# One gather of 96 slots for main and overflow tokens in a top-4-of-32 expert layer

## The chip, the cores and the metric
The kernel runs on one core of one Trainium2 chip. The metric is the device time of one execution in microseconds (us). A core has five engines with instruction streams of their own, TensorE (PE; its weight loads are listed apart as PEld), VectorE (DVE), ScalarE (ACT), GpSimd (POOL) and SyncE (SP), which wait for each other through semaphores. SyncE issues nearly all transfers here.

## The reference
One decoder layer for 256 tokens of 1024 values: an input projection, two kinds of attention, an output projection, a layer norm, and then a sparse feed-forward layer, which is what the change touches:

```
logits = h @ w_router + b_router          # 256 x 32
top_val, top_idx = top_k(logits, 4)
gates = softmax(top_val)
for each expert e, for its tokens:
    u = h @ w_up[e] + b_up[e]             # 1024 -> 2048, interleaved gate and up
    gate = min(u[::2], 7); up = clip(u[1::2], -7, 7)
    act = (up + 1) * gate * sigmoid(1.702 * gate)
    y[token] += gates * (act @ w_down[e] + b_down[e])
out = layer_norm(alpha * h + y)
```

All values are float32. An expert's weights are 12.58 MB (two halves of w_up and w_down, 4.19 MB each), all 32 experts' 403 MB.

## The kernel before
The first 235 us of the profiled execution hold the mixer and the router. The rest is one unrolled loop over the 32 experts, `for e in range(NE)` (L928), and then the second layer norm (`second_norm`, L1039).

**Slots.** Each expert has room for S = 64 tokens in its main pass. Tokens beyond that go to an overflow pass of Q = 32 slots, and a rare block, `general()` (L887), takes what exceeds 96 (and expert 0's overflow). `place` (L713) makes, from a token's rank among its expert's tokens, a 0/1 matrix `ph` (tokens by slots) on VectorE; `gather` (L736) multiplies the tokens, split in three bfloat16 parts (`hs`), with it on TensorE, 8 x 2 x 3 = 48 matmuls, and copies the result to `xg`, tokens' values by slots.

**One expert.** In the order of TensorE: `up` with the first half of w_up (L948); in odd experts `ways_back`; `up` with the second half (L961 or L968), each half of 32 matmuls of 512 columns by the profile; `swiglu` on VectorE and ScalarE beside it; the gather for the *next* expert (L978), whose copy VectorE makes; in even experts `combine`, which adds two experts' results to the four accumulators `y`; two transposes of `act` (L991) into `pts` (L988), one in the bank of `h0`, one in the two-deep ring `m`; the gates of the next expert's slots (`slot_gates`, L994) into the same bank as the second transpose; ScalarE's two copies to `actT` (L992, L995), the second behind the gates; then `down` (L1013) and its drain `keep_two` by ScalarE and VectorE.

**Conditionals.** Between the copies and `down` stands the first conditional, `is_over(e + 1)` (L1000): if the next expert overflows, place its overflow tokens, gather them, compute their gates, run `up` on the weights that are there and `swiglu`. Behind `down` stands the second, `is_over(e)` (L1019): place the way back on GpSimd (`place_back`), then `more_down` and `more_back`. Behind expert 30 stands the third, `words[4] > 0` (L1030), with the rare block of 32 conditionals with loops. Every engine has its own copy of each branch and tests a register of its own. The body of a conditional lies in the program behind the path that skips it: where it isn't entered, a branch goes past it.

**Weights.** Five slots of 4.19 MB form a ring (`ring`, L82). `load(k)` (L84) fills slot k % 5 with part k (three an expert) by SyncE; expert e issues the loads of parts 3e + 5 and 3e + 6, half by half, when `up` has read the part that was in the slot, and of part 3e + 7 behind both conditionals. The rare block reloads weights into one slot (`SLOT`, L926), the one of the down weights of the expert that it stands behind.

**PSUM.** Eight banks: four accumulators `y`, `h0`, `h1`, and the ring `m` of two, which the gather, the second transpose, `down` and others take in turn.

Of the kernel before, what the change touches and what calls it, by code (L numbers as in the profile page):

```python
# [9 lines left out]
F32 = mybir.dt.float32  # L10
# [21 lines left out]
def tile_hybrid(ctx, tc, x, w_in, w_o, lambda_qk, subln_g, sinks, ln_g, ln_b,  # L32
# [12 lines left out]
    def pool(stack, name, side="right", **kw):  # L45
# [2 lines left out]

    ident = keep.tile([128, 128], F32, name="ident")
    make_identity(nc, ident)  # L50
    iota_s = keep.tile([128, S], F32, name="iota_s")
    nc.gpsimd.iota(iota_s, pattern=[[1, S]], base=-int(NOT_HERE), channel_multiplier=0,
                   allow_small_or_imprecise_dtypes=True)
    iota_e = keep.tile([128, NE], F32, name="iota_e")
    nc.gpsimd.iota(iota_e, pattern=[[1, NE]], base=0, channel_multiplier=0, allow_small_or_imprecise_dtypes=True)
# [677 lines left out]
        nc.vector.tensor_reduce(gs, p, AX.X, OP.add)  # L733
        return gs

    def gather(ph, n, p=None, xg=None, copy=nc.scalar.copy):  # L736
        p = pm.tile([128, 8, n], F32, name="p", tag="m") if p is None else p
        for j in range(8):
            for tt in range(2):
                for k in range(3):  # L740
                    nc.tensor.matmul(p[:, j, :], hs[:, tt, k, j, :], ph[:, tt, :],  # L741
                                     start=(tt == 0 and k == 0), stop=(tt == 1 and k == 2))
        xg = mp.tile([128, 8, n], F32, name="xg", tag="xg") if xg is None else xg
        copy(xg, p)
        return xg

    halves = [slice(r * S, (r + 1) * S) for r in range(2)]
# [25 lines left out]
    def up(e, n, b, h, xg, u, js):  # L773

        G = 128 // n

        def cols16(t, q):
            o = 16 // G * q + 4 * b
            return t.rearrange("p (i r) -> p i r", r=16)[:, :, o:o + 4]

        if js[0] == 0:
            for q in range(G):
                nc.tensor.matmul(h[q * n:(q + 1) * n], sel[:, e:e + 1].to_broadcast([96, n]), cols16(bups, q),  # L783
                                 start=True, stop=False, tile_position=(0, q * n))
        for j in js:
            for q in range(G):
                nc.tensor.matmul(h[q * n:(q + 1) * n], xg[:, j, :], cols16(u[:, j % 4, :], q),  # L787
                                 start=False, stop=(j == 7), tile_position=(0, q * n))

    def swiglu(h, act, gs, tmp=None):  # L790
# [89 lines left out]
    gm3 = mp.tile([128, 2, NE, 3], BF, name="gm3", bufs=1)  # L880
    rankT = mp.tile([NE, 2, 128], BF, name="rankT", bufs=1)
    xg_of, gs_of = {}, {}
    ph = place(rankp[:, :, 0], S)
    xg_of[0] = gather(ph, S)
    ph_0 = ph
    nc.sync.dma_start(out=bd, in_=b_down[0])
    def general():  # L887

        d = ring[SLOT]
        df = d.rearrange("p j c -> p (j c)")  # L890
        act2 = mp.tile([128, 2, 128], F32, name="more")
        actT2 = mp.tile([128, 2, 128], F32, name="moreT", tag="actT0", bufs=1)
        yb2 = mp.tile([128, 512], F32, name="yb2", bufs=1)
        pgt2 = mp.tile([128, 2, 128], F32, name="pgt2", tag="actT1", bufs=1)
        pg2 = mp.tile([128, 2, 4, Q], F32, name="pg2", tag="pg", bufs=1)
        rk = mp.tile([128, 2], F32, name="rk")
        ph2 = mp.tile([128, 2, Q], BF, name=f"ph{Q}")
        xg2 = mp.tile([128, 8, Q], F32, name="xg", tag="xg")
        gs2 = mp.tile([128, 1], F32, name="gs")
        tmp = [mp.tile([128, 2, 128], F32, name=k, **kw) for k, kw in (("g", {"bufs": 1}), ("sg", {"bufs": 1}), ("u", {"bufs": 1}))]  # L900
        m = [pm.tile([128, 512], F32, name=f"m{k}", tag="m") for k in range(2)]
        three = [m[k].rearrange("p (a b) -> p a b", b=128)[:, 0:2] for k in range(2)]
        for e in range(NE):
            def again(i):
                nc.scalar.dma_start(out=df, in_=_rows(w_up, 128, e * D * 2048 + i * 8192, 16384, 8192))
                return d.rearrange("p (j a) c -> p j (a c)", a=2)

            with is_over(e, 1 if e else 0):
                nc.vector.tensor_scalar(rk, rankp[:, :, e], float(S if e else S - Q), None, op0=OP.subtract)
                n = nc.values_load(extra[:, e:e + 1], min_val=1, max_val=NX,  # L910
                                   skip_runtime_bounds_check_because="a count of at most 256 tokens")
                with tc.For_i(1 if e else 0, n, 1):
                    nc.vector.tensor_scalar(rk, rk, float(Q), None, op0=OP.subtract)
                    place_back(pg2, rk, 4, Q)
                    place(rk, Q, ph2)
                    gather(ph2, Q, m[0].rearrange("p (a b) -> p a b", b=Q)[:, 0:8], xg2)
                    slot_gates(ph2, e, Q, m[0][:, 256:259], gs2)
                    h2 = m[1].rearrange("p (i a b) -> p i a b", a=2, b=2)
                    for i in range(2):
                        up(e, Q, 0, h2, xg2, again(i), range(4 * i, 4 * i + 4))  # L920
                    swiglu(h2, act2, gs2, tmp)
                    nc.scalar.dma_start(out=df, in_=_rows(w_down, 128, e * D * D, 8192, 8192))
                    more_down(d, act2, actT2, pg2, pgt2, yb2, three + [m[0]])
                    more_back(pgt2, yb2)

    SLOT = (3 * (NE - 2) + 2) % 5  # L926
    act2_of = {}
    for e in range(NE):  # L928
        par = e % 2
        u0, u1, d = weights(e)  # L930
# [6 lines left out]
            elif k < 3 * NE:  # L937
                load(k, range(2 * half, 2 * half + 2), 4) if k > 3 * NE - 8 else load(k, (half,), 2)

        ph = place(rankp[:, :, e + 1], S) if e + 1 < NE else None  # L940
        if e == 0:
            counts()
            gates()
# [1 line left out]
        h = [h_tile(0), h_tile(1)]  # L945
        for j in range(4):
            for b in range(2):
                up(e, S, b, h[b], xg_of[e], u0, (j,))  # L948
            if j % 2:
                load_some(3 * e + 5, j // 2)  # L950
        if e == 0:
            turn_ranks()
            gs_of[0] = slot_gates(ph_0, 0, S, pm.tile([128, 3], F32, name="ps", tag="m"))
            words = [nc.values_load(over[:, k:k + 1], skip_runtime_bounds_check_because="a word of 16 flags")
                     for k in range(5)]
        if par == 1:
            wb = ways_back(e)
        if e < NE - 2:
            for b in range(2):
                for j in (4, 6):  # L960
                    up(e, S, b, h[b], xg_of[e], u1, (j, j + 1))  # L961
                    if b:
                        load_some(3 * e + 6, j // 2 - 2)
                swiglu(h[b], act[b], gs_of[e])
        else:
            for j in range(4, 8):
                for b in range(2):
                    up(e, S, b, h[b], xg_of[e], u1, (j,))  # L968
                if j % 2:
                    load_some(3 * e + 6, j // 2 - 2)  # L970
            for b in range(2):
# [3 lines left out]
            for k in range(2):  # L975
                nc.sync.dma_start(out=tail[:, k, :], in_=_rows((ln_g, ln_b)[k], 128, D, 0, D))
        if e + 1 < NE:
            xg_of[e + 1] = gather(ph, S, copy=nc.vector.tensor_copy)  # L978
        if par == 0 and e > 0:
            combine(wb)  # L980
        if e == NE - 1:
# [3 lines left out]
                for r in range(2):  # L985
                    nc.gpsimd.memset(part[halves[r], :, (1 - r) * 256:(2 - r) * 256].bitcast(F32), 0.0)  # L986
        actT = [mp.tile([128, 2, 128], F32, name=f"actT{b}", bufs=1) for b in range(2)]
        pts = [pm.tile([128, 512], F32, name="pt", tag="h0", bufs=1), pm.tile([128, 512], F32, name="pt", tag="m")]  # L988
        pt = [t[:, :256].rearrange("p (a b) -> p a b", b=128) for t in pts]
        for b in range(2):  # L990
            trans(act[b], pt[b])  # L991
        nc.scalar.copy(actT[0], pt[0])  # L992
        if e + 1 < NE:
            gs_of[e + 1] = slot_gates(ph, e + 1, S, pts[1][:, 256:259])  # L994
        nc.scalar.copy(actT[1], pt[1])  # L995
        if e == NE - 4:
            add_b_down()
# [1 line left out]
        if e + 1 < NE:  # L999
            with is_over(e + 1):  # L1000
                act2_of[e + 1] = mp.tile([128, 2, 128], F32, name="more")
                rk = mp.tile([128, 2], F32, name="rk")
                nc.vector.tensor_scalar(rk, rankp[:, :, e + 1], float(S), None, op0=OP.subtract)
                ph2 = place(rk, Q)
                p = pm.tile([128, 512], F32, name="p", tag="h0", bufs=1)
                xg2 = gather(ph2, Q, p[:, :256].rearrange("p (a b) -> p a b", b=Q))
                gs2 = slot_gates(ph2, e + 1, Q, p[:, 256:259])
                h2 = h_tile(0)
                for i, u in enumerate(weights(e + 1)[:2]):
                    up(e + 1, Q, 0, h2, xg2, u, range(4 * i, 4 * i + 4))  # L1010
                swiglu(h2, act2_of[e + 1], gs2)
        if e < NE - 1:
            p = down(d, S, actT, swap=par)  # L1013
# [3 lines left out]
            last_down(d, actT)  # L1017
        if e > 0:
            with is_over(e):  # L1019
                rk = mp.tile([128, 2], F32, name="rk")  # L1020
                nc.vector.tensor_scalar(rk, rankp[:, :, e], float(S), None, op0=OP.subtract)
                pg2 = mp.tile([128, 2, 4, Q], F32, name="pg2", tag="pg", bufs=1)
                place_back(pg2, rk, 4, Q)
                actT2 = mp.tile([128, 2, 128], F32, name="moreT", tag="actT0", bufs=1)
                yb2 = mp.tile([128, 512], F32, name="yb2", bufs=1)
                pgt2 = mp.tile([128, 2, 128], F32, name="pgt2", tag="actT1", bufs=1)
                more_down(d, act2_of[e], actT2, pg2, pgt2, yb2)
                more_back(pgt2, yb2)
        if e == NE - 2:
            with tc.If(words[4] > 0, preferred_fallthrough_block=False):  # L1030
                general()
        load(3 * e + 7)
# [53 lines left out]
```

## Time and profile before

| | us |
|---|---|
| median of 3 runs | 1237.45 (1232.15 to 1239.41) |
| profiled execution | 1235.14 |
| its span, first to last instruction | 1233.3 |
| TensorE matmuls busy | 1091.3 (88%) |
| VectorE, ScalarE, GpSimd busy | 364.1, 219.4, 104.0 |
| mean granted TensorE clock | 0.963 |
| read from memory | 438.72 MB, 357 GB/s over the span |

The span is what the trace covers; the execution's own time is 1.84 us more. Matmul ends are modelled, so a busy TensorE isn't TensorE at its peak. "issue" as the end of a wait means that the profile shows nothing that the engine waited for; an engine name with a q is that engine's sequencer, which branches and waits while the engine stands idle.

### The profile page before, as it was taken

The page shows a single profiled execution, that of the slowest core. Times are in us where ns is not written, and L with a number is a line of the kernel's source. Part 1 is how long each engine was busy: PE and PEld are TensorE (multiplying, and loading weights), DVE is VectorE, ACT ScalarE, POOL GpSimd, SP SyncE. Part 2 cuts the span into 40 slices and gives each one's busy share as a digit, 9 for nine tenths or more (in the row PEclk, how much of TensorE's full clock was granted, in tenths as well). Part 3 has the DMA queues.
Part 4 walks back from the last instruction along what each step waited for, and adds up shares of the span by engine and source line. Part 5 has one row for each costly group of instructions (what it writes and reads, how often), then busy time and mean ns, then how long its engine had stood idle before and what let it go on. Part 6 is the DMA issues. An engine that isn't in the chain of part 4 may idle for free. (4 is left out here: it accounts for less than half of the span.)

```text
span 1233.3 us, 17816 instructions
## 1 busy us (share of the span) xinstructions
PE 1091.3 (88%) x7027; PEld 545.3 (44%) x7027; DVE 364.1 (30%) x782; ACT 219.4 (18%) x458; POOL 104.0 (8%) x104
## 2 busy tenths in 40 slices
PE   8999999797999998779899998877899998898965
PEld 7989685332434343323343433332333433353322
DVE  4555964622122222111212122211122221222104
ACT  4765661301001001100001000000001100000001
POOL 1066561200000000000000000000000000000002
PEclk9999999899999999999999999989999999899988
DMA  9932537778899999997999999999999999999940
GB/s 333 380 123 104 196 113 297 297 295 368 337 408 426 425 425 425 412 399 323 375 425 425 426 426 425 427 425 428 426 424 426 426 426 427 424 425 420 418 180 35
DMA packets 46607, 441.80 MB, mean 358 GB/s; under 512 B 5121, under 2 KB 8321, under 8 KB 20513
## 3 DMA queue, kind: packets, MB, share of 16 engines
q1 hardware_dynamic: 46320, 439.52, 86.1%
q8 instruction: 104, 1.70, 0.6%
q14 instruction: 39, 0.31, 0.1%
q10 hardware_dynamic: 144, 0.26, 0.1%
HBM read 438.72 MB, written 1.05 MB: 357 GB/s over the span
## 5 line engine op out<-in xcount | busy, mean ns | idle before, releaser
L787 PE MATMUL h<-w,xg 128*64 128x512 f32 (+1 forms) x2176 | 476.5, 600 | 3.5 <-issue 2.4
L814 PE MATMUL pd<-w,actT 128*64 128x512 f32 x992 | 242.5, 638 | 64.5 <-issue 42.8
L787 PEld LDWEIGHTS h<-w,xg 128*64 128x64 f32 (+1 forms) x2176 | 167.0, 136 | 267.2 <-issue 255.2
L814 PEld LDWEIGHTS pd<-w,actT 128*64 128x64 f32 x992 | 84.9, 147 | 200.4 <-issue 184.3
L822 DVE TENSOR_TENSOR yl<-pd,yh 64x512 fp32r<-64x512 f32 (+1 forms) x66 | 44.4, 672 | 351.0 <-ACT yh L821 332.8
L796 ACT ACTIVATE sg<-g 128x256 f32<-128x256 f32 x66 | 27.6, 417 | 473.2 <-DVE g L795 473.2
L795 DVE TENSOR_SCALAR g<-h 128x256 f32<-128x256 f32 x66 | 28.0, 425 | 252.7 <-PE h L787 252.7
L821 ACT CAST yh<-pd 64x512 fp32r<-64x512 f32 (+1 forms) x66 | 37.4, 566 | 324.6 <-PE pd L814 294.1
L164 POOL TENSOR_TENSOR lo<-w,hi 128x1024 fp32r<-128x1024 f32 x31 | 78.9, 2553 | 103.4 <-ACT hi L163 103.3
L741 PEld LDWEIGHTS <-hs 128*128 128x128 bf16 x1632 | 50.3, 99 | 28.1 <-issue 24.5
L986 POOL MEMSET yh<- 64x512 f32 x2 | 1.0, 518 | 689.3 <-PE y L844 689.2
L741 PE MATMUL p<-ph,hs 128*128 128x64 bf16 (+1 forms) x1632 | 54.2, 194 | 2.8 <-DVE ph L717 2.8
L163 ACT CAST hi<-w 128x1024 fp32r<-128x1024 f32 x48 | 50.2, 1045 | 19.5 <-PE pj L202 13.8
L783 PE MATMUL h<-biases,sel 96*64 96x512 bf16 (+1 forms) x136 | 28.8, 410 | 27.6 <-ACT yh L821 16.4
L191 PE MATMUL pj<-xh,hi 128*128 128x256 f32 x272 | 40.8, 294 | 1.3 <-ACT gbt L516 0.7
L759 DVE TENSOR_SCALAR wb<-p,slot 128x512 fp32r<-128x512 f32 x16 | 12.0, 751 | 98.1 <-PE p L756 98.1
L191 PE MATMUL pj<-xl,hi 128*128 128x256 f32 x272 | 39.0, 287 | 0.0
L191 PE MATMUL pj<-xh,lo 128*128 128x256 f32 x272 | 39.0, 287 | 0.0
L191 PEld LDWEIGHTS pj<-xh,hi 128*128 128x128 f32 x272 | 36.0, 196 | 3.6 <-issue 1.0
L783 PEld LDWEIGHTS <-sel 96*64 96x64 bf16 (+1 forms) x136 | 9.3, 108 | 62.9 <-PEq L1019 41.6
L191 PEld LDWEIGHTS pj<-xh,lo 128*128 128x128 f32 x272 | 35.9, 196 | 0.0
L191 PEld LDWEIGHTS pj<-xl,hi 128*128 128x128 f32 x272 | 35.9, 196 | 0.0
(240 smaller groups left out, 829.1 us busy)
## 6 DMA issues: line engine op xcount, KB each, us to landing
w<-in_w_up_dram SPq DMA_DIRECT2D x120, 2048.0 KB, 22.3
w<-in_w_down_dram SPq DMA_DIRECT2D x58, 2048.0 KB, 23.2
w<-in_w_in_dram SPq DMA_DIRECT2D x5, 4096.0 KB, 15.6
w<-in_w_up_dram SPq DMA_DIRECT2D x16, 1024.0 KB, 21.2
w<-in_w_down_dram SPq DMA_DIRECT2D x12, 1024.0 KB, 20.8
w<-in_w_o_dram SPq DMA_DIRECT2D x2, 2048.0 KB, 10.9
w<-in_w_in_dram SPq DMA_DIRECT2D x1, 2048.0 KB, 14.4
w<-in_w_in_dram SPq DMA_DIRECT2D x1, 1536.0 KB, 9.6
```

The costliest lines, as they stand in the source:

```text
L163: nc.scalar.copy(hi, src)
L164: by.tensor_sub(lo, src, hi)
L191: nc.tensor.matmul(p[:, :256], a[:, j, :], b[:, j, :], start=(j == 0 and n == 0), stop=(j == 7 and n == 2))
L741: nc.tensor.matmul(p[:, j, :], hs[:, tt, k, j, :], ph[:, tt, :], start=(tt == 0 and k == 0), stop=(tt == 1 and k == 2))
L759: nc.vector.tensor_scalar(wb.rearrange("p k a b -> p k (a b)"), p, slot[:, 0:1], None, op0=OP.is_equal)
L783: nc.tensor.matmul(h[q * n:(q + 1) * n], sel[:, e:e + 1].to_broadcast([96, n]), cols16(bups, q), start=True, stop=False, tile_position=(0, ...
L787: nc.tensor.matmul(h[q * n:(q + 1) * n], xg[:, j, :], cols16(u[:, j % 4, :], q), start=False, stop=(j == 7), tile_position=(0, q * n))
L795: nc.vector.tensor_scalar(g, gt, 7.0, None, op0=OP.min)
L796: nc.scalar.activation(sg, g, AF.Sigmoid, scale=1.702)
L814: nc.tensor.matmul(p[r * n:(r + 1) * n, :w], actT[c // 2][:, c % 2, q * n:(q + 1) * n], d[:, k, o * w:(o + 1) * w], start=(k == 0), stop=( ...
L821: nc.scalar.copy(yh[at], p)
L822: nc.vector.tensor_sub(yl[at], p, yh[at])
```

## The change
The gather of an expert makes S + Q = 96 columns in place of 64, so that the overflow tokens are gathered along with the others, for every expert, whether it overflows or not. Its result takes two banks of the ring `m` (four groups of 96 columns, at a pitch of 128, in each) and two copies; the gathered tile is single, not double. The first conditional loses its placement and its gather, and gets the `place_back` of the second. The second transpose moves from the ring `m` to the bank of `h1`. The rare block moves from behind expert 30 to behind expert 24 (`LATE`), and some tiles of the blocks get other buffers.

```diff
-    def gather(ph, n, p=None, xg=None, copy=nc.scalar.copy):
-        p = pm.tile([128, 8, n], F32, name="p", tag="m") if p is None else p
-        for j in range(8):
+    def gather(ph, p):
+        for j, pj in enumerate(p):
             for tt in range(2):
                 for k in range(3):
-                    nc.tensor.matmul(p[:, j, :], hs[:, tt, k, j, :], ph[:, tt, :],
+                    nc.tensor.matmul(pj, hs[:, tt, k, j, :], ph[:, tt, :],
                                      start=(tt == 0 and k == 0), stop=(tt == 1 and k == 2))
-        xg = mp.tile([128, 8, n], F32, name="xg", tag="xg") if xg is None else xg
-        copy(xg, p)
+
+    def gather_all(ph, copy):
+        p = [pm.tile([128, 4, 128], F32, name="p", tag="m") for k in range(2)]
+        gather(ph, [p[j // 4][:, j % 4, :S + Q] for j in range(8)])
+        xg = mp.tile([128, 8, S + Q], F32, name="xg", bufs=1)
+        for k in range(2):
+            copy(xg[:, 4 * k:4 * k + 4], p[k][:, :, :S + Q])
         return xg
...
-    SLOT = (3 * (NE - 2) + 2) % 5
-    act2_of = {}
+    LATE = 24
+    SLOT = (3 * LATE + 2) % 5
+    act2_of, pg2_of = {}, {}
...
-        ph = place(rankp[:, :, e + 1], S) if e + 1 < NE else None
+        ph = place(rankp[:, :, e + 1], S + Q) if e + 1 < NE else None
+        xg = [xg_of[e][:, j, :S] for j in range(8)]
...
-            xg_of[e + 1] = gather(ph, S, copy=nc.vector.tensor_copy)
+            xg_of[e + 1] = gather_all(ph, nc.vector.tensor_copy)
...
-        pts = [pm.tile([128, 512], F32, name="pt", tag="h0", bufs=1), pm.tile([128, 512], F32, name="pt", tag="m")]
+        pts = [pm.tile([128, 512], F32, name="pt", tag=f"h{b}", bufs=1) for b in range(2)]
...
             with is_over(e + 1):
                 act2_of[e + 1] = mp.tile([128, 2, 128], F32, name="more")
+                pg2_of[e + 1] = mp.tile([128, 2, 4, Q], F32, name="pg2")
                 rk = mp.tile([128, 2], F32, name="rk")
                 nc.vector.tensor_scalar(rk, rankp[:, :, e + 1], float(S), None, op0=OP.subtract)
-                ph2 = place(rk, Q)
-                p = pm.tile([128, 512], F32, name="p", tag="h0", bufs=1)
-                xg2 = gather(ph2, Q, p[:, :256].rearrange("p (a b) -> p a b", b=Q))
-                gs2 = slot_gates(ph2, e + 1, Q, p[:, 256:259])
+                place_back(pg2_of[e + 1], rk, 4, Q)
                 h2 = h_tile(0)
                 for i, u in enumerate(weights(e + 1)[:2]):
-                    up(e + 1, Q, 0, h2, xg2, u, range(4 * i, 4 * i + 4))
+                    up(e + 1, Q, 0, h2, [xg_of[e + 1][:, j, S:] for j in range(8)], u, range(4 * i, 4 * i + 4))
+                gs2 = slot_gates(ph[:, :, S:], e + 1, Q, pm.tile([128, 3], F32, name="p", tag="h1", bufs=1))
                 swiglu(h2, act2_of[e + 1], gs2)
...
             with is_over(e):
-                rk = mp.tile([128, 2], F32, name="rk")
-                nc.vector.tensor_scalar(rk, rankp[:, :, e], float(S), None, op0=OP.subtract)
-                pg2 = mp.tile([128, 2, 4, Q], F32, name="pg2", tag="pg", bufs=1)
-                place_back(pg2, rk, 4, Q)
...
-                more_down(d, act2_of[e], actT2, pg2, pgt2, yb2)
+                more_down(d, act2_of[e], actT2, pg2_of[e], pgt2, yb2)
                 more_back(pgt2, yb2)
-        if e == NE - 2:
+        if e == LATE:
             with tc.If(words[4] > 0, preferred_fallthrough_block=False):
                 general()
```

## Rows read from the trace of the kernel before

**Rows 1.** The page: one DMA queue (packets, MB, share of 16 engines).
```profile
q8 instruction: 104, 1.70, 0.6%
```

**Rows 2.** Waits, whole span (who <- whom: us in total, times, longest).
```profile
PE pd L814 <- issue: 42.8, 13, 6.5
PE h L783 <- issue: 8.4, 1, 8.4
PE pd L814 <- DMA w<-in_w_up_dram: 6.6, 1, 6.6
PE h L787 <- DMA w<-in_w_up_dram: 1.0, 1, 1.0
...
SPq L99 <- PE h L787: 315.1, 95, 9.1
```

**Rows 3.** Branches of L1000, L1019, L1030 on TensorE (ns min/median/max, first and last us).
```profile
L1000 PEldq COMPARE_BRANCH  x60: 66/238/6142, 256.6 to 1171.5; - x60
L1019 PEldq COMPARE_BRANCH  x60: 66/187/404, 300.4 to 1221.9; - x60
L1030 PEldq COMPARE_BRANCH  x2: 71/3614/7157, 1182.5 to 1183.0; - x2
```

**Rows 4.** Windows around entered blocks (first, second, first): busy us (x instructions) by engine.
```profile
257.95:269.28 11.33, 10.46 (x124) 3.89 (x124) 0.24 (x2) 0.37 (x1) 0.00 (x0) 0.85 0.67 282
303.60:317.95 14.35, 9.29 (x79) 4.32 (x80) 3.22 (x8) 2.26 (x5) 1.20 (x2) 0.88 0.36 133
468.60:479.44 10.84, 8.97 (x124) 3.51 (x124) 0.28 (x2) 0.37 (x1) 0.00 (x0) 1.00 1.01 425
```

**Rows 5.** Timeline of TensorE, four starts of an expert, one gather, one hole.
```profile
675.49 0.42 PE L783 MATMUL h<-biases,sel 96*64 96x512 bf16 x2 [0.73 <-ACT yh L821]
...
702.39 0.42 PE L783 MATMUL h<-biases,sel 96*64 96x512 bf16 x2 [0.73 <-ACT yh L821]
...
717.20 1.57 PE L741 MATMUL p<-ph,hs 128*128 128x64 bf16 x48
...
728.41 0.42 PE L783 MATMUL h<-biases,sel 96*64 96x512 bf16 x2 [0.73 <-ACT yh L821]
...
749.39 8.56 PE L814 MATMUL pd<-w,actT 128*64 128x512 f32 x32 [2.55 <-issue]
...
758.68 0.42 PE L783 MATMUL h<-biases,sel 96*64 96x512 bf16 x2 [0.73 <-ACT yh L821]
```

**Rows 6.** Windows: the same columns, then clock, DMA share, GB/s.
```profile
549.00:553.30 4.30, 0.00 (x0) 0.00 (x0) 0.00 (x0) 0.00 (x0) 0.00 (x0) 0.73 0.99 419
553.30:558.00 4.70, 4.63 (x12) 1.62 (x14) 0.00 (x0) 0.00 (x0) 0.00 (x0) 0.52 0.69 289
235.00:345.00 110.00, 98.18 (x738) 39.88 (x740) 28.63 (x94) 13.49 (x27) 1.20 (x2) 0.94 0.83 343
520.00:600.00 80.00, 65.35 (x416) 27.20 (x418) 14.19 (x34) 6.20 (x14) 0.00 (x0) 0.91 0.85 350
600.00:1180.00 580.00, 518.20 (x3227) 218.52 (x3225) 123.82 (x287) 53.60 (x118) 0.00 (x0) 0.96 1.00 423
```

**Rows 7.** Groups by line and shape: VectorE's drain (busy us, mean ns).
```profile
L744 DVE COPY xg<-p 128x512 f32<-128x512 f32 x31 | 21.2, 685 | 0.0
```

**Rows 8.** Timeline in the two blocks that are entered for one expert.
```profile
258.03 1.35 PE L741 MATMUL p<-ph,hs 128*128 128x32 bf16 x48 [1.07 <-DVE ph L717]
...
260.39 0.41 PE L783 MATMUL h<-biases,sel 96*32 96x512 bf16 x4 [0.34 <-DVE gs L733]
...
308.36 0.42 DVE L767 COPY pgt<-p 128x256 f32<-128x256 f32 x1 [1.72 <-PE p L765]
```

**Rows 9.** Timeline and one window of the tail.
```profile
1200.95 7.09 PE L787 MATMUL h<-w,xg 128*64 128x512 f32 x32
...
1221.88 1.30 DVE L1041 BATCH_NORM_STATS2 st<-y 128x6 f32<-128x512 f32 x2 [0.92 <-PEq L1019]
...
1188.00:1192.00 4.00, 1.66 (x6) 0.74 (x8) 0.00 (x0) 0.00 (x0) 0.00 (x0) 0.50 0.34 132
```

More of the change, by code (lines that the diff above doesn't have):

```diff
@@ L50, in tile_hybrid @@
     make_identity(nc, ident)
-    iota_s = keep.tile([128, S], F32, name="iota_s")
-    nc.gpsimd.iota(iota_s, pattern=[[1, S]], base=-int(NOT_HERE), channel_multiplier=0,
+    iota_s = keep.tile([128, S + Q], F32, name="iota_s")
+    nc.gpsimd.iota(iota_s, pattern=[[1, S + Q]], base=-int(NOT_HERE), channel_multiplier=0,
                    allow_small_or_imprecise_dtypes=True)
@@ L786, in up @@
             for q in range(G):
-                nc.tensor.matmul(h[q * n:(q + 1) * n], xg[:, j, :], cols16(u[:, j % 4, :], q),
+                nc.tensor.matmul(h[q * n:(q + 1) * n], xg[j], cols16(u[:, j % 4, :], q),
                                  start=False, stop=(j == 7), tile_position=(0, q * n))
@@ L882, in tile_hybrid @@
     xg_of, gs_of = {}, {}
-    ph = place(rankp[:, :, 0], S)
-    xg_of[0] = gather(ph, S)
-    ph_0 = ph
+    ph_0 = place(rankp[:, :, 0], S + Q)
+    xg_of[0] = gather_all(ph_0, nc.scalar.copy)
     nc.sync.dma_start(out=bd, in_=b_down[0])
@@ L894, in general @@
         pgt2 = mp.tile([128, 2, 128], F32, name="pgt2", tag="actT1", bufs=1)
-        pg2 = mp.tile([128, 2, 4, Q], F32, name="pg2", tag="pg", bufs=1)
+        pg2 = mp.tile([128, 2, 4, Q], F32, name="pg2")
         rk = mp.tile([128, 2], F32, name="rk")
         ph2 = mp.tile([128, 2, Q], BF, name=f"ph{Q}")
-        xg2 = mp.tile([128, 8, Q], F32, name="xg", tag="xg")
+        xg2 = mp.tile([128, 8, Q], F32, name="xg2", tag="act0", bufs=1)
         gs2 = mp.tile([128, 1], F32, name="gs")
@@ L915, in general @@
                     place(rk, Q, ph2)
-                    gather(ph2, Q, m[0].rearrange("p (a b) -> p a b", b=Q)[:, 0:8], xg2)
+                    p = m[0].rearrange("p (a b) -> p a b", b=Q)[:, 0:8]
+                    gather(ph2, [p[:, j] for j in range(8)])
+                    nc.scalar.copy(xg2, p)
                     slot_gates(ph2, e, Q, m[0][:, 256:259], gs2)
@@ L919, in general @@
                     for i in range(2):
-                        up(e, Q, 0, h2, xg2, again(i), range(4 * i, 4 * i + 4))
+                        up(e, Q, 0, h2, [xg2[:, j, :] for j in range(8)], again(i), range(4 * i, 4 * i + 4))
                     swiglu(h2, act2, gs2, tmp)
@@ L947, in tile_hybrid @@
             for b in range(2):
-                up(e, S, b, h[b], xg_of[e], u0, (j,))
+                up(e, S, b, h[b], xg, u0, (j,))
             if j % 2:
@@ L952, in tile_hybrid @@
             turn_ranks()
-            gs_of[0] = slot_gates(ph_0, 0, S, pm.tile([128, 3], F32, name="ps", tag="m"))
+            gs_of[0] = slot_gates(ph_0[:, :, :S], 0, S, pm.tile([128, 3], F32, name="ps", tag="m"))
             words = [nc.values_load(over[:, k:k + 1], skip_runtime_bounds_check_because="a word of 16 flags")
@@ L960, in tile_hybrid @@
                 for j in (4, 6):
-                    up(e, S, b, h[b], xg_of[e], u1, (j, j + 1))
+                    up(e, S, b, h[b], xg, u1, (j, j + 1))
                     if b:
@@ L967, in tile_hybrid @@
                 for b in range(2):
-                    up(e, S, b, h[b], xg_of[e], u1, (j,))
+                    up(e, S, b, h[b], xg, u1, (j,))
                 if j % 2:
@@ L993, in tile_hybrid @@
         if e + 1 < NE:
-            gs_of[e + 1] = slot_gates(ph, e + 1, S, pts[1][:, 256:259])
+            gs_of[e + 1] = slot_gates(ph[:, :, :S], e + 1, S, pts[1][:, 256:259])
         nc.scalar.copy(actT[1], pt[1])
@@ L1019, in tile_hybrid @@
             with is_over(e):
-                rk = mp.tile([128, 2], F32, name="rk")
-                nc.vector.tensor_scalar(rk, rankp[:, :, e], float(S), None, op0=OP.subtract)
-                pg2 = mp.tile([128, 2, 4, Q], F32, name="pg2", tag="pg", bufs=1)
-                place_back(pg2, rk, 4, Q)
                 actT2 = mp.tile([128, 2, 128], F32, name="moreT", tag="actT0", bufs=1)
```

## The prediction

> **What bounds the kernel now.** I read the waits first. TensorE hardly ever waits for weights: the longest wait that is truly one is 1.0 us [rows 2]. The transfers wait for TensorE instead: the queue that loads weights sat 315.1 us until the up matmuls had freed a slot [rows 2]. So the order of work on TensorE sets the end, and its holes are worth their length, until the weights themselves come too late.
>
> The holes have one place. Thirteen times the down projection (L814) started after a wait that nothing in the profile explains, 42.8 us together, and a fourteenth of 6.6 us is put down to a transfer [rows 2]. They stand directly behind the first conditional of an expert (L1000), or some matmuls into the down projection that follows it. The branch rows say what it is: TensorE's branch there lasts 0.24 us at the median and 6.142 us at the longest; at the second conditional (L1019) the same two branches never last over 0.404 us; at the rare block (L1030) one took 7.157 us [rows 3]. A branch that is not entered skips its block. A taken first block holds 124 matmuls and 124 weight loads (two experts of 31 enter it, at 258 and at 469 us), a second one about 76 of each, beside three or four strays of its neighbours [rows 4]. The instructions come from memory in packets of 16 KB (1.70 MB in 104) [rows 1]; the long skip often lands where they have not arrived.
>
> The windows show what follows a hole: during the wait of 549 to 553.3 us the granted clock fell to 0.73 in the mean, and in the 4.7 us behind it it was 0.52, so TensorE ran at its 1.2 GHz level after having stood idle [rows 6]. From 600 to 1180 us the clock is 0.96, from 520 to 600 us 0.91 [rows 6]. Without a hole an expert takes 26.9 us (675.49 to 702.39) or 26.0 (to 728.41); with one of 2.55 us it took 30.3 (to 758.68) [rows 5].
>
> Behind this limit lies a second one. An expert's weights are 12.58 MB, which at 423 to 426 GB/s is 29.6 us, more than TensorE's 26.5. From 600 to 1180 us the transfers are at a share of 1.00, but from 520 to 600 us at 0.85 and from 235 to 345 us at 0.83, where TensorE was late with slots [rows 6]. They end shortly before 1190 us [rows 9], and TensorE ends 32 us later: it runs some 26 us behind what the weights allow.
>
> **The change part by part.** The sum is made against the profiled span of 1233.3 us.
>
> *Shorter skip.* The gather's 48 loads and 48 matmuls leave the first block: 248 instructions become 152, the length of the second block, whose skips (29 experts, no branch over 0.404 us) show no stall [rows 3, 4]. I therefore take the 49.4 us of waits as gone. Bounds: nothing gone, and all. The low clock behind them goes too: 0.04 x 580 + 0.09 x 80 = 30 us of lost full speed, of which a third lies inside the waits (0.27 x 4.3 = 1.2 us against 0.48 x 4.7 = 2.3 us in the rows), so 20 us. Bounds 0 and 30. Together 69 us of TensorE time.
>
> The Trainium skill, "Runtime: NRT & Kernel Launch", section "Instruction fetch mechanics", says that an engine holds only a small window of blocks of its instructions and that a taken branch to outside of it waits for a fetch. By that rule alone a skip of 152 still leaves a block often, so the stalls would shrink by length and not vanish; the rows of L1019 speak against it, and I give it a rival below.
>
> *Wider gather.* It makes 96 columns for each expert where it made 64. 48 matmuls took 1.35 us at 32 columns [rows 8] and 1.57 us at 64 [rows 5]: the next 32 cost at least 0.22 us again, and at most half of 1.57, 0.79. I take 0.6, near the top, as the columns weigh more the wider they are: 31 x 0.6 = 19 us of TensorE time (7 to 24).
>
> *Two drains instead of one.* VectorE copied 512 columns in 0.685 us [rows 7] and 256 in 0.42 [rows 8]; two copies of 384 lie between, 0.55 each, 0.42 us more than before. Queued behind them on VectorE is the sum of the gates, behind that ScalarE's second transposed copy, and the down projection waits for that copy. But the gather ends 0.6 us later anyway, so nearly the same delay is counted once; without that cover it is 0.4 x 31 = 13 us. Both banks of the ring are now held by the gather; the second transpose, which stood in one of them, goes to the other up bank, whose readers must have finished before its operand exists: nothing. The down projection takes the bank that is drained first, before its own operand is copied: nothing, else 0.55 per expert. The single gathered tile is written only after the last matmul that reads it, by order of TensorE: nothing.
>
> *The two blocks that are entered* (experts 1 and 8). In the first, the block's bias matmul came at 260.39 us, behind a placement, the gather from 258.03, its copy and the gates [rows 8]; without them it can begin near 257.8: 2.6 us each. In the second the placement on GpSimd is done already, so the copy at 308.36 [rows 8] can come some 1.9 us earlier. 2 x 4.5 = 9 us. GpSimd's placement now lies beside the 11 us of the first block's matmuls; if that cover were gone it costs the 1.9 again.
>
> *The rare block* goes from behind expert 30, where its skip held TensorE for 8.4 us with no weights missing [rows 2], to behind expert 24. There the skip costs the same 7.2 us branch [rows 3] and makes the load that follows it late; but at that point the loads of all of the next expert and of half the one behind it are issued already, of which some 29.6 us are still to be moved when TensorE waits for weights; and TensorE, being faster, makes up 29.6 - 27.1 = 2.5 us per expert over six experts. So 8.4 us go and nothing comes; if TensorE still sets the pace, 7.2 come back.
>
> Sum on TensorE: 1233.3 - 69 - 8.4 - 9 + 19 = 1166 us. That is below what the weights allow, so the second limit decides. Transfers: last landing 1190, less the 12 us that were lost from 520 to 600 us (0.15 x 80), where TensorE is now some 20 us earlier; the 19 us lost from 235 to 345 give perhaps 2, since TensorE there gains 4 and pays 1 to 2 (bounds 0 and 5). So 1176. Behind the last landing the tail is fixed: the last up weights land a down projection's 9.9 us earlier (4.19 MB); then the last quarter of 7.09 us of up matmuls, 1.8; from the end of those at 1208.0 to the end of the span, 25.3: 1.8 + 25.3 - 9.9 = 17.2 us [rows 9]. (That counts from the last up weights; the down weights' last quarter, landing at the end, has less behind it.) 1176 + 17 = 1193. TensorE now idles a little at each weight; should its clock drop in the last expert, 28 matmuls cost 1 to 2 us more, at most 6. I put 2: span 1195. The profiled execution took 1.84 us beyond its span (1235.14), and the median of the runs, 1237.45, lies 2.3 above that; half of this added gives 1198.
>
> **The rivals.**
> *The stalls shrink by length only.* 152/248 = 0.61 of the 69 us stay: 1233.3 - 27 - 8.4 - 9 + 19 = 1208, and as TensorE then has no slack at expert 24 the 7.2 comes back: 1215, a time of 1218. For it: landing places are spread over a block, and 152 is no small part of 248. Against: no second conditional stalled. But those come behind 7 us of slow down matmuls, the first ones 3 us behind a gather that consumes 96 instructions in 1.6 us, and that is why it keeps a real chance.
> *The stall belongs to the jump, not to its length*, and all 69 stay: 1233.3 + 19 - 9 - 8.4 + 7.2 = 1242, time 1245: slower. It decides as soon as less than 9 of the 69 us go. Against: the same jump at L1019 is cheap 29 times.
> *The transfers hide it.* They are at 1.00 for most of the time, so nothing would change. Against: TensorE is 26 us behind them at the end, with 8.4 us of pure wait in the tail.
>
> **How the numbers follow.** Forecast, transfers set the end: 0.72, own range 1186 to 1206 (first stretch 5 us better and no low clock; drains uncovered and some stalls left). Shrinking by length 0.15, staying 0.07, hidden 0.04, neither 0.02. A difference of 0.5%, 6 us, is about what a measurement of this kernel can tell from none. Faster 0.88, same 0.04, slower 0.08. The range takes in the first rival: 1184 to 1222.
>
> **What would show it.** Right: TensorE's branch at L1000 stays under half a microsecond, the unexplained waits before L814 vanish, waits of the up matmuls for weights appear in the last ten experts, transfers are at 1.00 from 345 us to near 1176, the long branch of L1030 stands near 950 us. The gather's 48 matmuls take 2.0 to 2.4 us. Wrong: branches of 2 to 6 us at L1000 or now at L1019, no waits for weights at all, or experts of over 29 us without a hole.

## The result, and the profile of the changed kernel

The changed kernel took 1196.49 us in the median of 4 runs (1195.11 to 1198.51), the kernel before 1238.43 in the same measurement: a ratio of 0.9672, 95% interval 0.9636 to 0.9709. The forecast was 1198, the range 1184 to 1222. The profiled execution took 1196.55 us with a span of 1194.8 (forecast 1195), at a mean granted clock of 0.98.

The waits of the changed kernel (who <- whom: us in total, times, longest):

```profile
PE h L792 <- DMA w<-in_w_up_dram: 23.5, 14, 3.0
PE h L788 <- issue: 8.0, 1, 8.0
...
SPq L99 <- PE h L792: 212.0, 66, 8.8
...
SPq L1033 <- SPq L1033: 39.3, 2, 34.4
```

All fourteen waits before the down projection, 49.4 us [rows 2], are gone. In their place stand fourteen waits of the up matmuls for weights, 23.5 us together, and the loads wait 212.0 us for TensorE where they waited 315.1. The last row is one that the prediction doesn't speak of: SyncE stood 39.3 us inside the conditional of the rare block (now L1033), 34.4 of them in one wait. The kernel before has the same row, much smaller:

```profile
SPq L1030 <- SPq L1030: 10.4, 4, 4.4
```

The branches of the changed kernel at the first and second conditional and at the rare block (ns, least, median, most; first and last us):

```profile
L1008 PEldq COMPARE_BRANCH  x60: 66/182/391, 256.4 to 1146.5; - x60
L1026 PEldq COMPARE_BRANCH  x60: 66/178/397, 292.4 to 1183.5; - x60
L1033 PEldq COMPARE_BRANCH  x2: 71/3484/6897, 968.9 to 969.3; - x2
```

The first conditional is now like the second: its longest branch fell from 6.142 us [rows 3] to 0.391. The rare block's long branch stands at 969 us and is as long as before.

Windows of the changed kernel (busy us of PE, PEld, DVE, ACT, POOL with instructions; clock, DMA share, GB/s):

```profile
235.00:345.00 110.00, 103.29 (x730) 43.63 (x732) 30.97 (x98) 14.07 (x28) 1.20 (x2) 0.97 0.90 371
520.00:600.00 80.00, 76.44 (x488) 31.33 (x488) 18.54 (x44) 7.63 (x17) 0.00 (x0) 1.00 1.00 419
600.00:900.00 300.00, 276.74 (x1741) 116.49 (x1740) 72.18 (x169) 28.78 (x63) 0.00 (x0) 0.99 1.01 425
985.00:1010.00 25.00, 23.68 (x158) 9.91 (x156) 7.00 (x16) 2.74 (x6) 0.00 (x0) 1.00 0.64 258
```

Against [rows 6], the stretch of 520 to 600 us is full, as forecast; that of 235 to 345 gained 0.07 x 110 = 7.7 us of transfers, where 2 were forecast; and 985 to 1010 has a hole of 0.36 x 25 = 9 us that was not forecast. Its origin is in the timeline of SyncE's load issues (start, us from the first to the end of the last, count):

```profile
954.16 49.23 SPq L99 DMA_DIRECT2D w<-in_w_up_dram  x4
1003.49 0.93 SPq L99 DMA_DIRECT2D w<-in_w_down_dram  x2
```

Four loads that follow each other take 49 us to be issued. The second goes out at 958.6 us; then SyncE enters the conditional, and it leaves it at 999.6, 0.4 us after the last load issued before had landed (999.2). The next load starts at 1002.5 and lands at 1011.4. In the kernel before SyncE left the conditional at 1192.9 us, also 0.4 us after its last load had landed. The wait is one that the program makes: SyncE has nine semaphore instructions in this conditional, and none in the first two.

```profile
L1033 SPq EVENT_SEMAPHORE  x9: 17/17/17, 959.9 to 999.6; - x9
```

TensorE's timeline in the changed kernel, the first entered block, three starts of an expert, one gather, and expert 28:

```profile
257.26 7.05 PE L792 MATMUL h<-w,xg 128*32 128x512 f32 x64
...
264.27 7.09 PE L819 MATMUL pd<-w,actT 128*64 128x512 f32 x32
...
470.02 2.84 PE L792 MATMUL h<-w,xg 128*32 128x512 f32 x16 [2.89 <-DMA w<-in_w_up_dram]
...
680.54 0.42 PE L788 MATMUL h<-biases,sel 96*64 96x512 bf16 x2 [0.44 <-PEq L1026]
...
695.35 2.21 PE L740 MATMUL p<-ph,hs 128*128 128x96 bf16 x48
...
706.53 0.42 PE L788 MATMUL h<-biases,sel 96*64 96x512 bf16 x2 [0.62 <-PEq L1026]
...
733.84 0.61 PE L788 MATMUL h<-biases,sel 96*64 96x512 bf16 x2 [0.44 <-PEq L1026]
...
1075.13 7.01 PE L792 MATMUL h<-w,xg 128*64 128x512 f32 x24 [2.96 <-DMA w<-in_w_up_dram]
...
1087.63 3.69 PE L709 MATMUL y<-biases,gT 32*128 32x512 f32 x8 [0.51 <-DVEq L1008]
1091.99 8.78 PE L819 MATMUL pd<-w,actT 128*64 128x512 f32 x32 [0.66 <-PEq L1008]
```

The gather's 48 matmuls take 2.21 us, in the forecast 2.0 to 2.4, yet two experts take 733.84 - 680.54 = 53.3 us against 52.9 before [rows 5]: 0.2 us each for the wide gather with all that came with it. The wait at 1075 is the last one for weights. From there to the end TensorE runs without one.

### The profile page after: what moved, and what is told of

It reads as the page before. It is cut to its first block, busy times and chain, and to the rows that moved or that the text cites. A ratio compares the mean times of both kernels' runs of the same rounds, so it can differ in the third digit from the quotient of the medians.

```text
span 1194.8 us, 17658 instructions
## 1 busy us (share of the span) xinstructions
PE 1087.2 (91%) x6931; PEld 544.0 (46%) x6931; DVE 373.9 (31%) x807; ACT 219.0 (18%) x457; POOL 104.0 (9%) x104
## 5 line engine op out<-in xcount | busy, mean ns | idle before, releaser
L792 PE MATMUL h<-w,xg 128*64 128x512 f32 (+1 forms) x2176 | 480.7, 603 | 25.3 <-DMA w<-in_w_up_dram 23.5
L792 PEld LDWEIGHTS h<-w,xg 128*64 128x64 f32 (+1 forms) x2176 | 151.8, 137 | 308.2 <-issue 261.9
L819 PE MATMUL pd<-w,actT 128*64 128x512 f32 x992 | 222.1, 600 | 18.8 <-ACTq L1008 13.0
L819 PEld LDWEIGHTS pd<-w,actT 128*64 128x64 f32 x992 | 82.2, 138 | 134.7 <-issue 114.7
L740 PEld LDWEIGHTS <-hs 128*128 128x128 bf16 x1536 | 67.7, 99 | 25.9 <-issue 23.4
L740 PE MATMUL p<-ph,hs 128*128 128x96 bf16 x1536 | 72.3, 208 | 0.7 <-DVE ph L717 0.7
```

The costliest lines, as they stand in the source:

```text
L740: nc.tensor.matmul(pj, hs[:, tt, k, j, :], ph[:, tt, :], start=(tt == 0 and k == 0), stop=(tt == 1 and k == 2))
L792: nc.tensor.matmul(h[q * n:(q + 1) * n], xg[j], cols16(u[:, j % 4, :], q), start=False, stop=(j == 7), tile_position=(0, q * n))
L819: nc.tensor.matmul(p[r * n:(r + 1) * n, :w], actT[c // 2][:, c % 2, q * n:(q + 1) * n], d[:, k, o * w:(o + 1) * w], start=(k == 0), stop=( ...
```

## The experiments

**How long the skip is.** Three kernels put matmuls that nobody reads back into one conditional's block and leave the wide gather, the banks and the rare block's place as changed.

```diff
+                spare = pm.tile([128, 4, 128], F32, name="p", tag="h0", bufs=1)
+                gather(ph[:, :, S:], [spare[:, j % 4, :Q] for j in range(8)])   # range(4): 24 matmuls
                 h2 = h_tile(0)
```

48 matmuls in the first conditional: 

> The changed kernel with 48 matmuls of 32 columns put back into the first conditional's block, into a bank that nobody reads, so that the skip is 248 instructions again while the wide gather, the banks and the rare block's place stay. Theory (length of the skip): the unexplained waits before L819 come back, 13 or so of 2 to 6 us, some 49 us and 20 us of low clock; TensorE's sum of 1166 + 69 + 7 + 3 = 1245 passes the transfers' 1195, so 1225 to 1245 us. Rival (the waits went for another reason: the other bank, the gates and the placement that left, a shift of all addresses): no such waits, 1197 to 1200 us (2 x 1.35 us for the two blocks that are entered).

24 matmuls there: 

> The changed kernel with 24 spare matmuls in the first conditional's block: a skip of 200 instructions, half way between 152 and 248. If the stall goes by length in proportion, about half of the 38 us that the 96 instructions brought back: 1210 to 1222 us, with some 7 unexplained waits. If there is a length below which nothing stalls, and it lies above 200, 1197 to 1200 us without such waits; if it lies below, nearly all, 1228 to 1236 us.

48 matmuls in the second conditional's block: 

> The changed kernel with the 48 spare matmuls in the second conditional's block instead of the first's: its skip becomes 250 instructions, the first stays at 152. If the length alone decides, the second conditional (L1026 of the changed kernel) now stalls as the first did: branches of 2 to 6 us in about half of the experts, waits of some 45 us ahead of the next expert's first matmul, 1225 to 1240 us. Rival, which the prediction weighed (what stands ahead of the branch decides: 7 us of slow down matmuls there, a gather that uses up 96 instructions in 2 us ahead of the first): few or short stalls, 1197 to 1210 us.

Measured: 1234.48 us (ratio to the kernel before 0.9997, interval 0.9968 to 1.0027), 1204.26 (0.9738, 0.9702 to 0.9774) and 1219.10 (0.9863, 0.9828 to 0.9897). The branch and then the waits of the first kernel, 248 instructions:

```profile
L1008 PEldq COMPARE_BRANCH  x60: 66/236/6249, 256.2 to 1180.6; - x60
```

```profile
PE pd L819 <- issue: 44.2, 14, 6.6
...
PE pd L819 <- DMA w<-in_w_up_dram: 4.6, 1, 4.6
```

Of the second, 200 instructions:

```profile
L1008 PEldq COMPARE_BRANCH  x60: 66/187/3107, 257.2 to 1154.8; - x60
```

```profile
PE pd L819 <- issue: 14.2, 8, 3.5
```

Of the third, some 250 instructions in the second conditional (L1026):

```profile
L1008 PEldq COMPARE_BRANCH  x60: 66/187/387, 257.4 to 1172.0; - x60
...
L1026 PEldq COMPARE_BRANCH  x60: 66/229/6436, 293.2 to 1208.9; - x60
```

```profile
PE h L788 <- issue: 38.3, 5, 14.4
...
PE h L792 <- issue: 7.8, 3, 4.1
```

With 96 instructions back in the block, the branch, the waits (48.8 us against 49.4) and the time are those of the kernel before: the whole gain is gone with the long skip, though the wide gather, the transpose and the rare block's place stay as changed. These three together weigh nothing here; each of them need not, as the move of the rare block alone made the kernel before faster (below). At 200 instructions fewer waits remain and they are shorter, 14.2 us; 1204 us fits none of the three cases expected. At 152 there are none: the price falls faster than the length. The third kernel moves the stall to the other conditional, out of the first. Less the skip of the rare block (8.0 us elsewhere), its waits are 38.3 + 7.8 - 8.0 = 38 us, and 4 more are put down to VectorE; they stand at nine experts, where about half of the 31 were expected. 1219 us lies in neither range, 6 us below the 1225 to 1240 of the theory and 9 above the 1197 to 1210 of the rival. So what stands ahead of the branch does not protect a skip of this length; why fewer of them stall there than at the first conditional was not followed.

What the skip waits for can be read from the transfers. The queue of instructions moves packets of 16 KB [rows 1], one in some 10 us. In the kernel before, each of the fourteen waits ahead of or inside the down projection ends 1.3 to 1.7 us after such a packet has landed, the one put down to a transfer of weights too. With 96 instructions back it is so for all fifteen, and at 200 for the seven that last over 1 us. The changed kernel's waits for weights keep no such distance: they end anywhere from 0.1 to 10.6 us after one. A block that isn't entered is moved all the same: the queue has 104 packets at 248 instructions, in the kernel before and in the first of the three, and fewer when the block is shorter. First 200 instructions, then the changed kernel:

```profile
q8 instruction: 98, 1.61, 0.5%
q8 instruction: 94, 1.54, 0.5%
```

**Where the rare block stands.**

```diff
-    LATE = 24
+    LATE = 30      # and 31, and no conditional at all
```

Behind expert 30: 

> The changed kernel with the rare block back behind expert 30 (`LATE = 30`); all else as changed. The prediction's step on the move (8.4 us go, nothing comes) expects those 8.4 us back in the tail, and nothing in exchange: 1196.5 + 8.4 = 1205 us. The rival, formed from the trace of the changed kernel: the skip at expert 24 costs what it saves, since SyncE stood 34 us in it until every issued load had landed, and the transfers ran at a share of 0.64 from 985 to 1010 us, 0.36 x 25 = 9 us lost. By it the tail wait comes back but the transfers end 9 us sooner: 1196 us (1193 to 1199), with the transfers at a share of 1.00 from 985 to 1010 us and the last weights landing near 1168.

Left out: 

> The changed kernel without the conditional of the rare block; it leaves out the tokens beyond 96 of an expert and beyond 64 of expert 0. The prediction's step (nothing comes at expert 24) expects no change, 1196.5 us. The rival (the skip at expert 24 drains the queue of loads) expects 9 us less, 1187 to 1188 us, and no gap in the transfers between 985 and 1010 us.

Behind expert 31: 

> The changed kernel with the rare block behind the last expert (`LATE = 31`), where all loads have landed and TensorE has nothing left to do but the skip. Theory, from the two places run so far: behind expert 30 the skip cost TensorE a wait of 8.0 us and 2.4 us of low clock behind it, behind expert 24 it cost the transfers 7 to 9 us; behind expert 31 neither is paid, as TensorE signals ahead of the long branch (its semaphores stand before it) and nobody waits for TensorE behind it: the span of the run at 30, 1199.7, less 8.0 and 2.4, 1189 us, a time near 1192. Rival: VectorE, ScalarE and SyncE must pass the conditional too before the layer norm, or wait for TensorE's branch, and the tail grows by up to 7 us: 1199.

In the kernel before, that move alone: 

> The kernel before with one part of the change alone: the rare block behind expert 24 in place of 30; the gather stays inside the first conditional. The prediction's step gives 8.4 us for the move where transfers set the end, and 8.4 less 7.2 back, 1 us, where TensorE does. Here TensorE sets the pace (it waits for no weights), so by that step no difference, 1237 us (1235 to 1239). Rival (SyncE's wait for all issued loads costs transfers here as well): the lost transfers make TensorE wait for weights behind expert 24, 1240 to 1246 us.

Measured: 1202.26 us (0.9744, 0.9707 to 0.9780), 1192.89 (0.9643, 0.9614 to 0.9671), 1194.78 (0.9672, 0.9646 to 0.9697), and for the last 1226.10 (0.9926, 0.9899 to 0.9952). Neither theory of the first two held by itself: 1202 lies between 1205 and 1196, 1193 between 1196.5 and 1187.5. The kernel without the block shows the hold gone. In its timeline of SyncE the same four loads are issued within 15 us, and in its windows the transfers are full from 985 to 1010 us:

```profile
954.22 15.02 SPq L99 DMA_DIRECT2D w<-in_w_up_dram  x4
```

```profile
985.00:1010.00 25.00, 19.81 (x117) 7.56 (x115) 3.72 (x9) 1.95 (x5) 0.00 (x0) 0.96 1.01 425
```

So the hold and the hole belong to the conditional. Expert 28, the last that waits for weights, then starts its up matmuls at 1055.92 in place of 1062.48 us: 6.6 us of the 9 arrive there. In that expert 3.0 are lost again (42.23 us to the next start against 39.18), in a longer stretch of low clock, and 3.4 of span are left. The kernel with the block behind expert 30 shows the price of the old place; its timeline of TensorE, and its windows:

```profile
1156.95 0.64 PE L788 MATMUL h<-biases,sel 96*64 96x512 bf16 x2 [8.04 <-issue]
```

```profile
1152.00:1158.00 6.00, 1.05 (x4) 0.46 (x6) 0.00 (x0) 0.00 (x0) 0.00 (x0) 0.50 0.83 312
1158.00:1162.00 4.00, 4.00 (x12) 1.09 (x10) 0.00 (x0) 0.00 (x0) 0.00 (x0) 0.50 0.66 221
```

TensorE stands for 8.04 us and then works at its 1.2 GHz level; from the first up matmul of expert 31 to the end of the span it takes 42.3 us against 39.9. By the medians the old place costs 1202.26 - 1192.89 = 9.4 us, the new one 1196.49 - 1192.89 = 3.6, and the move brings 5.8 (by the spans 1199.7, 1194.8 and 1191.4: 8.3, 3.4 and 4.9; against the later median of the changed kernel, 1197.92, the move brings 4.3).

Behind expert 31 the expectation was 1192. TensorE's branch is hidden there, but VectorE now skips the block just ahead of the layer norm (timeline; the same row of the changed kernel under it in the next fence):

```profile
1181.65 1.30 DVE L1044 BATCH_NORM_STATS2 st<-y 128x6 f32<-128x512 f32 x2 [3.50 <-issue]
```

```profile
1183.39 1.30 DVE L1044 BATCH_NORM_STATS2 st<-y 128x6 f32<-128x512 f32 x2 [0.92 <-PEq L1026]
```

That is 2.6 us more, the sign of the rival and some third of its size. By the medians the time can hardly be told from that of the changed kernel. But the two profiled executions differ ahead of the loop already, where the edit changes nothing: the same matmul (L646) starts at 236.93 us here and at 234.67 in the changed kernel. From there to the end they take 956.1 and 960.1 us (960.0 in the second profile of the changed kernel), 4 us less where 4.5 were expected.

The move alone in the kernel before was expected to change nothing, and made it 0.74% faster. SyncE is held there too (34.8 us in one wait), and the transfers run at a share of 0.67 from 1010 to 1040 us; but the waits for weights that the rival asked for did not come (one of 0.9 us), as TensorE is that far behind. What changed is the stalls:

```profile
PE pd L814 <- issue: 35.7, 12, 4.5
...
PE h L783 <- issue: 8.3, 1, 8.3
...
PE pd L814 <- DMA w<-in_w_up_dram: 6.1, 1, 6.1
```

The rare block's skip still costs 8.3 us, but the others fell from 49.4 to 41.8. Of these 7.6 us, 4.3 lie behind the new place, where the stalls now stand at experts 25, 26 and 27 (at 1024, 1058 and 1093 us; before at 26, 27, 29 and 30, at 1041, 1072, 1140 and 1177). The other 3.3 lie ahead of it, in the same code and at the same experts: the skip whose wait ends at 814 us cost 6.50 us in the one execution and 3.27 in the other. So a skip's price changes from one execution to the next, and whether moved code shifts where the skips stall can't be told from one profile of each. The 7.6 stand against 9.8 us between the two spans (1233.3 and 1223.5); the rest was not followed.

**Who sets the end.** A gather of 64 columns (the other edits left out here only adapt its slices):

```diff
-        gather(ph, [p[j // 4][:, j % 4, :S + Q] for j in range(8)])
+        gather(ph[:, :, :S], [p[j // 4][:, j % 4, :S] for j in range(8)])
```

> The changed kernel with a gather of 64 columns in place of 96, still into two banks with two copies of 256; the first conditional stays short, as its matmuls read the main slots, so the overflow tokens get wrong values. Theory (the transfers set the end): the same time within 3 us, 1194 to 1198 us, and TensorE waits longer for weights by about what the gather saves, 0.2 to 0.6 us an expert. Rival (TensorE still sets the end, the wide gather is paid in full): 7 to 19 us less, 1178 to 1190 us.

And with the rare block behind expert 31, the bias of the down projections eight experts earlier, run beside the changed kernel itself:

```diff
-        if e == NE - 4:
+        if e == 20:
             add_b_down()
```

> The kernel with the rare block behind expert 31, and the bias of the down projections (`add_b_down`) at expert 20 in place of 28. Theory (up to expert 28 the weights set the pace, behind it TensorE does: it loses some 10 us in expert 28 to `add_b_down` and the low clock behind it, and is still 3.9 us behind the last up weights in expert 31): at expert 20 the 5 us are hidden under the transfers, expert 28 takes 32 us in place of 41, and the end comes 3 to 4 us sooner, 1190.5 to 1192 us. Rival (the end is the last landing, 1172, and a fixed tail, whatever expert 28 does): the same as with the rare block at 31 alone, 1194.8.

> The changed kernel itself, nothing edited, as the reference for the two beside it: 1196 to 1197 us.

Measured: 1194.14 us for the narrow gather (0.9662, 0.9627 to 0.9697), 1191.46 (0.9656, 0.9620 to 0.9693) with the bias at expert 20, and 1197.92 (0.9698, 0.9661 to 0.9735) for the changed kernel beside it. In the kernel with the narrow gather, the gather's group (busy us, mean ns), and the waits:

```profile
L740 PE MATMUL p<-ph,hs 128*128 128x64 bf16 x1536 | 51.5, 195 | 0.7 <-DVE ph L717 0.7
```

```profile
PE h L792 <- DMA w<-in_w_up_dram: 30.7, 15, 3.8
...
PE pt L808 <- DVE act L804: 5.3, 17, 1.3
```

It saves 0.64 us an expert, 20 in all; TensorE waits 7.2 us longer for weights and 4.0 longer for `act` (1.3 in the changed kernel), and 2.3 us reach the time (3.8 against 1197.92); the remaining 5 to 7 us were not followed. So most of it is hidden, as expected, over half of it in these two waits. But the transfers do not set the very end: moving 5 us of TensorE's work out of expert 28, where it had no wait to hide under, brought 1194.78 - 1191.46 = 3.3 us, from two measurements; counted from the same matmul (L646), the profiled executions take 956.1 and 953.4 us, 2.7 less. This version beats both kernels: 6.5 us below the changed one beside it, five of its six runs (1189.41 to 1191.75) below the fastest of the other (1194.48).

**The second transpose back in the ring.**

```diff
-        pts = [pm.tile([128, 512], F32, name="pt", tag=f"h{b}", bufs=1) for b in range(2)]
+        pts = [pm.tile([128, 512], F32, name="pt", tag="h0", bufs=1), pm.tile([128, 512], F32, name="pt", tag="m")]
```

> The changed kernel with one part undone: the second transpose back in the ring `m`, now behind the two banks of the gather. The prediction's step (it costs nothing where it stands) holds that the place of this transpose is worth nothing by itself; back in the ring it must wait for VectorE's first drain, and the down projection for the second. Theory: 0 to 0.55 us of TensorE an expert, hidden under the transfers up to expert 28, so 1196 to 1198 us. Rival (the other bank is what the change lives on: without it the waits for the drains chain up, the full 1.1 us an expert and more): 1203 or over, with waits of the transposes or of the down projection for VectorE's copies.

Measured 1196.93 us (0.9697, 0.9662 to 0.9732), beside 1197.92 for the changed kernel: no difference, and no wait of a transpose or a down projection for a drain appears.

## Why the prediction was right, and where it was not

**Shorter skip: right.** All 49.4 us of waits went, as taken. Of the two readings of [rows 3], the one that trusted the second conditional's skips held, and the rival that gave 0.61 of the stalls to 152 instructions fell: none are left there, and even 200 keep only 14.2 us. The Trainium skill, "Runtime: NRT & Kernel Launch", "Instruction fetch mechanics", says that a taken branch to outside the loaded blocks waits for a fetch; the stalls at 200 and 248, which end 1.3 to 1.7 us after a packet of instructions, agree with it, and what it does not give, how the price runs with length, is 0, 14.2 and 48.8 us here.

**Wider gather and drains: right in size.** 2.21 - 1.57 = 0.64 us an expert (0.6 taken), two drains of 0.548 us (0.55 taken). The sum overlooked that the transposes were waiting for `act` anyway: the wide gather fills that wait, so an even and an odd expert together grew by 0.8 us from the narrow gather to the wide one, not by 1.3.

**Entered blocks: right in the sum.** From the last twelve up matmuls ahead of it to the down projection behind it, the stretch of the first block took 17.6 us before (251.70 to 269.29) and 12.8 now (251.44 to 264.27): 4.8 less with the wider gather paid, where 2.6 - 0.6 were forecast; 1.7 of the rest is the block's 64 matmuls, 8.75 before and 7.05 now; the second conditional took 1.3 less (1.9 forecast). At the second overflow the block's up matmuls wait 2.89 us for weights, so nothing is gained there: from the gather to the down projection it took 14.3 us before and takes 14.8; its second conditional took 1.2 less. In all that is 6.8 us, where 9 less 1.2 for the gathers were forecast.

**First stretch: mis-sized.** The step "the 19 us lost from 235 to 345 give perhaps 2" (bounds 0 and 5) measured 7.7. Its sum left out the stall of 1.78 us at 300 and the low clock of that stretch (0.94, now 0.97); expert 2 starts its up matmuls 8.5 us sooner (309.60 against 318.06), so the slots are freed that much sooner.

**Rare block: the step that failed.** "So 8.4 us go and nothing comes" was wrong twice. At expert 24 the loads on their way did cover TensorE's skip, as it said; but SyncE itself was held in the conditional until all of them had landed, so none was issued for 44 us and the transfers lost 9. The row of SyncE's wait at L1030, 10.4 us, stood in the trace of the kernel before, and the prediction makes nothing of it. And at expert 30 more went than the 8.4: the low clock behind the skip cost 2.4. The move brought 4 to 6.

**Transfers set the end: right in the number, half right in the mechanism.** The last weights landed at 1176.7 us, 1176 forecast: 5.7 us more gained in the first stretch against 9 lost at expert 24, and most of the rest is 425 GB/s in place of 423. The span behind that was 18.1 us, 19 taken. But the last wait for weights is at 1075 us. From expert 28 on TensorE sets the end, because `add_b_down` and the slow matmuls behind it made expert 28 39 us long. In expert 31 the matmuls on the last quarter of the up weights start 1.3 us after these have landed (1167.2 and 1165.9), those on the last quarter of the down weights 2.5 us after (1179.2 and 1176.7). That the sum came out within 2 us is in part luck: an error of 5.7 us and one of 9 went against each other, and the two limits ended within 3 us of each other. The experiment with the bias shows that TensorE held the last of it.

## What to carry to other kernels

Count the instructions that a conditional skips: a body cut from 248 to 152 was worth 38 us here, though the work taken out of it was done 31 times instead of twice. Before a rarely entered block with transfers in it is moved to where "everything is issued already", ask which engine's queue must pass it, and read its waits at the old place: the one that issues the loads may be held until they have all landed. When two limits lie close, put the work that one engine must do once where the other limit hides it; eight experts earlier brought about 3 us here, and expert 28 started no later for it.

## What the runs showed of the hardware that was not expected

TensorE's clock fell without TensorE standing idle. Behind `add_b_down` (8 matmuls that use 32 of 128 rows, with gaps of at most 0.7 us around them), the windows of the kernel with the bias at expert 20 show it at the new place:

```profile
838.00:841.00 3.00, 2.49 (x16) 1.60 (x15) 0.58 (x2) 0.74 (x2) 0.00 (x0) 1.00 1.00 426
841.00:846.00 5.00, 4.48 (x7) 1.21 (x6) 0.00 (x0) 0.00 (x0) 0.00 (x0) 0.63 1.01 428
846.00:851.00 5.00, 4.84 (x16) 1.73 (x18) 0.00 (x0) 0.00 (x0) 0.00 (x0) 0.68 1.03 433
851.00:856.00 5.00, 4.33 (x22) 1.39 (x20) 0.63 (x1) 0.58 (x1) 0.00 (x0) 1.00 1.00 426
```

TensorE was busy for 9.3 of those 10 us and still ran part of them at its 1.2 GHz level. At expert 28 the changed kernel shows 0.76 and 0.81 in the same place, and the kernel without the rare block 0.50 for 5 us, which is where 3 of its 6.6 us went. The fall goes where `add_b_down` goes: the changed kernel, which has it at expert 28, shows 1.00 from 841 to 851 us, and with it at expert 20 the down matmuls of expert 28 (1080 to 1090 us) run at 1.00. Whether the few rows are the cause was not tried.

VectorE pays for a long skip too: 2.6 us ahead of the layer norm with the rare block behind expert 31, and in the changed kernel the placement behind L1033 waits 6.2 us, where it waits 0.3 in the kernel without the rare block. That wait costs nothing: the gather that reads the placement comes 17 us later.
